# Layer 1's first operands beside projection 0's last block: SBUF pools laid out by the end of their place, PSUM pools kept over both parts

## The chip, the core and the metric

One Trainium2 chip, one of its cores. The metric is the device time of one execution in microseconds (us); lower is better. In the profile PE is TensorE, DVE VectorE, ACT ScalarE, POOL GpSimd and SP the engine that issues the DMAs.

## The reference

One inference step of a two-layer backbone over 128 prompt and 2048 latent tokens, width 1024. What matters here is the end of layer 0 and the start of layer 1:

```python
h = rmsnorm(x, norm_g[l]) * (1.0 + scale) + shift
# l == 0: gated linear attention heads | spatial-gating heads -> out (T x 1024)
# l == 1: pooling mixer heads | short gated convolution heads -> out (T x 1024)
out = out @ w_out[l]
x = x + gate * out
```

Layer 0's output projection ("projection 0") gives x after layer 0; layer 1 normalizes that x, multiplies it with an input projection of 1024 x 3072, mixes, and projects again.

## The kernel before, in words

Everything is kept channel-major: 128 channels on the partitions, tokens along the free axis. A float32 product is made from two halves, a rounded high part and the remainder (lines 206 to 208: ACT copies the high half, DVE or POOL subtracts for the low half), and three matmuls each (line 238).

Projection 0 (`out0`, line 1050) goes over five blocks of tokens (`BLKO`, line 31), called blocks 0 to 4 here: 512, 512, 512, 384 and 256 tokens. A block has eight output columns `c` of 128 channels; each takes 24 matmuls into one PSUM bank `ps_g`, DVE empties the bank into `xs_y` (line 1059), ACT squares it, POOL adds the squares (line 292), and a DMA writes `d_x1`. After a block, its inverse root mean square goes to `d_r` (line 1068). The weights of columns 0 to 2 lie in pool `wp`, those of columns 3 to 7 in `wr`. The operands of a block, `oh` and `ol`, lie in pool `oA` (blocks 0, 2, 4) or `oB` (blocks 1, 3). They are finished in tiles of 128 tokens by `finish_o` (line 911) while the block before is multiplied: load, add the state's product, sum of squares on TensorE (lines 270, 271), `newton` (lines 262 to 266), scale (lines 967, 968), split (line 971). Every tile but tile 0 also needs a state from the scan backwards (line 905).

Layer 1 (`block`, line 1446) goes over four blocks of 544 tokens, last tokens first, so that its first block needs x of tokens 1624 to 2175 only, which projection 0 has written with its second block. `operand` (line 1146) makes the block's operands: per `k` of 4 it loads two pieces `xk` of `d_x1`, scales them with `r` (line 372), adds the shift on ACT (line 1160), forms four differences `T` on POOL and DVE (line 1172) and splits seven tiles `t` into halves, 28 in all. The product is a Winograd form of seven products for each pair of weight rows (`Pair`, line 1378): m1, m2, m5, m6 of a pair, with m7, m4, m3 of the pair before between them. Then the output projection of the block (lines 1511 to 1538), whose banks line 1529 empties.

The order on each engine is set by the framework's scheduler from the program's dependences. A tile of a pool that is opened later waits only for those tiles of the closed pools on whose bytes it lies (`reuse_waits="tile"`). So where a pool lies decides when its first tile may be written. In the program before, `xk` lies on `oB`; the 28 tiles `t` lie on `oB` (10 of them), `wr` and a part of `xs`; `r` and `T` lie on the last `y` and `x` tiles of `xs`, which are in use to the end of projection 0. The PSUM pools `ps2` (4 banks `g`, 2 `m`, 2 `s`) and `ps3` (6 banks `g`, 2 `s`) follow each other.

Of the kernel before, what the change touches and what calls it, by code (L numbers as in the profile page):

```python
# [10 lines left out]
F32 = mybir.dt.float32  # L11
# [18 lines left out]

BLKO = [(1664, 2176), (1152, 1664), (640, 1152), (256, 640), (0, 256)]
NBO = len(BLKO)
# [54 lines left out]
def kernel(ctx: ExitStack, tc: tile.TileContext, xT, cT, w_ada, b_ada, norm_g, final_g,  # L87
# [29 lines left out]
    def const(src, shape, tag, dt=F32, pl=None):  # L117
        t = (pl or cst).tile(shape, dt, tag=tag)
        load(out=t, in_=src)
        return t  # L120

    def mtile():

        return ps.tile([P, 2, 512], F32, tag="m", bufs=banks[0])

    def btile():
        return (ps.tile([P, 512], F32, tag="m", bufs=2) if banks[0] == 1 else mtile()[:, 0, :])

# [782 lines left out]
    def finish_o(bi):  # L911
# [8 lines left out]
        def ob_part():  # L920
            for hh in range(4):
                hi, lo = o_tile(n, bi % 2)
                x = (xs.tile([P, WOP], F32, tag="x", bufs=2) if bi else
                     tmp.tile([P, 640], F32, tag="px", bufs=2))[:, 0:n]
# [101 lines left out]
    s2 = ExitStack()  # L1026
    ps = pool("ps2", space=PSUM, stack=s2, reuse_waits="tile")
    banks[:] = BANKS2
    opools.append(pool("oB", stack=s2, reuse_waits="tile"))
    wr = pool("wr", stack=s2, reuse_waits="tile")  # L1030
    xs = pool("xs2", stack=s2, reuse_waits="tile")
    tmp = pool("tmp2", stack=s2, reuse_waits="tile")
    width[:] = [512, 0, 0, 0, 3, 6]

# [3 lines left out]
    def w_out0(c):  # L1038
        if c == len(wres):
            if c < NHI:  # L1040
                wres.append(load_w(wo[0, c], KT * P))
            else:
                raw = raw_tile()[:, 0:KT * P]
                load(out=raw, in_=wo[0, c])
                hi, lo = (wr.tile([P, KT * P], F32R, tag=f"{z}{c}") for z in "hl")
                split(raw, hi, lo)
                wres.append((hi, lo))
        return wres[c]
# [36 lines left out]
    s3 = ExitStack()  # L1085
    ps = pool("ps3", space=PSUM, stack=s3, reuse_waits="tile")
    banks[:] = BANKS3
    wh = pool("wh", stack=s3, reuse_waits="tile")
    ring = pool("ring2", stack=s3, reuse_waits="tile")
    tmp = pool("tmp3", stack=s3, reuse_waits="tile")  # L1090
    c3 = pool("c3", stack=s3, reuse_waits="tile")
    late = ExitStack()
    o1 = pool("o1", stack=late, reuse_waits="tile", right=True)
# [50 lines left out]
    kept = [None]  # L1144

    def operand(bi, c0, w):

        jw = w - HALF
        r = tmp.tile([P, 560], F32, tag="r", bufs=1)[:, 0:w]
        load(out=r, in_=d_r[:, c0:c0 + w])  # L1150
        B = {n: [] for n in ("B11", "B21", "T1", "B22", "T2", "T3", "T4")}
        cn = cond_ranges(c0, c0 + w)
        for k in range(4):
            h = []
            for kk in (k, k + 4):
# [23 lines left out]
    def in1(bi, o8, fill):  # L1179
# [107 lines left out]
        def pair_pool(hh):  # L1287
# [17 lines left out]
            def c12(x, y):  # L1305
# [12 lines left out]
                for s0_, sn, off, lft, rgt in own_segs:  # L1318
# [59 lines left out]
        class Pair:  # L1378
# [67 lines left out]
    def block(bi):  # L1446
# [218 lines left out]
```

## Time and profile before

| | |
|---|---|
| median of 3 runs | 1901.35 us (1898.92 to 1901.35) |
| the profiled execution's own time | 1904.74 us |
| its span | 1902.9 us |
| TensorE busy | 1756.3 us, 92% of the span |
| VectorE busy | 1193.6 us, 63% |
| ScalarE busy | 842.0 us, 44% |
| GpSimd busy | 745.8 us, 39% |
| DMA engines | 69.3% of 16 engines' span |

The durations below come from the one profiled execution; 1.8 us lie around its span, and its time is 3.4 us above the median. TensorE is busy nearly everywhere, so the places where it is not are what to look for. The span in slices shows where they are, the stretches show how much they cost, the chain and the timelines show what they wait for.

### The profile page before, as it was taken

To read this page: it belongs to the slowest core of one execution; us is meant where nothing else is said; L and a number is where in the kernel's file an instruction comes from. 1 tells how busy PE (TensorE), PEld (TensorE's weight loads), DVE (VectorE), ACT (ScalarE), POOL (GpSimd) and SP (SyncE) were. 2 spreads that over 40 slices of the span, in tenths; PEclk is the share of its full clock that TensorE was granted. 3 is DMA by queue.
4 is the path that set the end of the run, shared out by engine and by line. 5 is a ranking of instruction groups with operands and counts; after the bars stand their busy time and mean duration, and the time that the engine had idled before them with its cause. 6 is when DMAs were issued, how large, how long until landed. Compare 5 with 4: busy or idle time off the path is not lost.

```text
span 1902.9 us, 39872 instructions
## 1 busy us (share of the span) xinstructions
PE 1756.3 (92%) x15115; PEld 1595.2 (84%) x15115; DVE 1193.6 (63%) x2262; ACT 842.0 (44%) x1783; POOL 745.8 (39%) x796
## 2 busy tenths in 40 slices
PE   5998999989988998998899959999999999999996
PEld 3886778768876987987678949988999999999996
DVE  4657853882588348646775456585768476837663
ACT  3545542542454436434444444454445254534431
POOL 0432433550474223244554343354346334532322
PEclk9999899989988999999899969999999999999998
DMA  8767796878867574475755367777877597759762
GB/s 310 269 234 244 271 319 225 280 270 285 284 227 247 205 264 148 145 210 174 218 168 162 111 199 251 247 246 241 313 266 253 177 325 250 235 180 327 236 213 98
DMA packets 232319, 443.76 MB, mean 233 GB/s; under 512 B 26176, under 2 KB 69056, under 8 KB 232128
## 3 DMA queue, kind: packets, MB, share of 16 engines
q1 hardware_dynamic: 232128, 441.22, 69.3%
q8 instruction: 119, 1.95, 0.4%
q14 instruction: 72, 0.59, 0.1%
HBM read 344.44 MB, written 96.68 MB: 232 GB/s over the span
## 4 chain that ended last, share of the span: by engine, by line
PE 59%; DVE 18%; DMA 12%; issue 4%; ACT 3%; SPq 2%; POOL 1%; DVEq 0%; ACTq 0%; POOLq 0%
PE ps_g L238 54%; DVE gl_Z L546 2%; DVE ring_xk L372 2%; DMA wp_raw<-in_w0c_dram 2%; DVE ring_t L208 2%; DMA wa_wa<-in_w_ada_dram 1%; DVE gl_L L535 1%; DMA dr_hl<-tmp_px 1%; DMA ring_xk<-dr_x 1%; DVE oA_Sb L905 1%; DMA oA_Sb<-dr_ub 1%; PE ps_s L338 1%; PE ps_s L1335 1%; DVE wp_raw L735 1%; DVE gl_A L598 1%
## 5 line engine op out<-in xcount | busy, mean ns | idle before, releaser
L238 PE MATMUL ps_g<-ring_t,wh_hi 128*128 128x272 f32 (+1 forms) x2688 | 525.7, 295 | 20.1 <-ACT ring_t L207 12.4
L238 PEld LDWEIGHTS ps_g<-ring_t,wh_hi 128*128 128x128 f32 x2688 | 428.7, 191 | 26.7 <-ACT ring_t L207 13.6
L238 PE MATMUL ps_g<-ring_t,wh_lo 128*128 128x272 f32 (+1 forms) x1344 | 387.9, 293 | 0.7 <-DVE wh_lo L208 0.7
L238 PEld LDWEIGHTS ps_g<-ring_t,wh_lo 128*128 128x128 f32 x1344 | 254.5, 191 | 1.5 <-DVE wh_lo L208 1.2
L238 PE MATMUL ps_g<-ring_hh,wp_hi 128*128 128x512 f32 (+2 forms) x632 | 239.1, 378 | 11.1 <-DVE tmp_ev L847 5.8
L238 PE MATMUL ps_g<-ring_hh,wp_lo 128*128 128x512 f32 (+2 forms) x632 | 235.3, 372 | 4.8 <-DVE wp_lo L208 3.9
L238 PE MATMUL ps_g<-ring_hl,wp_hi 128*128 128x512 f32 (+2 forms) x632 | 234.0, 370 | 0.0
L207 ACT ACTIVATE wh_hi<-wh_raw 128x512 fp32r<-128x512 f32 x208 | 130.7, 629 | 209.1 <-PE ps_g L238 175.5
L292 POOL TENSOR_TENSOR tmp_acc<-tmp_acc,tmp_px 128x512 f32<-128x512 f32 (+6 forms) x83 | 112.1, 1351 | 154.6 <-ACT tmp_px L291 152.7
L208 DVE TENSOR_TENSOR wh_lo<-wh_raw,wh_hi 128x512 fp32r<-128x512 f32 x156 | 125.5, 808 | 64.9 <-ACT wh_hi L207 50.4
L238 PE MATMUL ps_g<-wp_hi,ring_hh 128*128 128x256 f32 (+1 forms) x528 | 157.3, 299 | 8.2 <-DMA wp_hi<-dr_w8h 3.4
L238 PE MATMUL ps_g<-wp_lo,ring_hh 128*128 128x256 f32 (+1 forms) x528 | 152.5, 290 | 1.2 <-DMA wp_lo<-dr_w6l 0.8
L238 PE MATMUL ps_g<-wp_hi,ring_hl 128*128 128x256 f32 (+1 forms) x528 | 152.2, 290 | 1.1 <-DVE ring_hl L388 1.1
L238 PE MATMUL ps_g<-o_oh,wh_hi 128*128 128x272 f32 (+2 forms) x512 | 147.0, 292 | 5.9 <-ACT o_oh L207 5.9
L546 POOL TENSOR_TENSOR gl_Z<-gl_Z 128x128 f32<-128x128 f32 x170 | 84.0, 512 | 173.7 <-DVE gl_Z L546 106.4
L238 PE MATMUL ps_g<-o_ol,wh_hi 128*128 128x272 f32 (+2 forms) x512 | 149.5, 293 | 1.5 <-DVE o_ol L208 1.4
L238 PEld LDWEIGHTS ps_g<-ring_hh,wp_hi 128*128 128x128 f32 x632 | 123.9, 196 | 31.8 <-DVE tmp_ev L847 6.2
L238 PE MATMUL ps_g<-o_oh,wh_lo 128*128 128x272 f32 (+2 forms) x512 | 149.2, 292 | 0.8 <-DMA wh_lo<-dr_wo 0.8
L238 PEld LDWEIGHTS ps_g<-ring_hh,wp_lo 128*128 128x128 f32 x632 | 123.3, 195 | 24.3 <-DVE wp_lo L208 5.3
L238 PEld LDWEIGHTS ps_g<-ring_hl,wp_hi 128*128 128x128 f32 x632 | 123.7, 196 | 16.0 <-issue 1.2
L530 ACT ACTIVATE gl_L<-gl_Z 128x256 f32<-128x256 f32 x204 | 83.2, 418 | 110.8 <-DVE gl_Z L546 83.3
L238 PEld LDWEIGHTS ps_g<-wp_hi,ring_hh 128*128 128x128 f32 x528 | 101.7, 193 | 15.1 <-ACT ring_hh L387 4.0
(280 smaller groups left out, 3910.1 us busy)
## 6 DMA issues: line engine op xcount, KB each, us to landing
wh_raw<-in_w_dram SPq DMA_DIRECT2D x144, 256.0 KB, 3.6
wh_hi<-dr_hl SPq DMA_DIRECT2D x144, 256.0 KB, 3.3
wh_lo<-dr_hl SPq DMA_DIRECT2D x144, 256.0 KB, 3.7
wp_raw<-in_w_ada_dram SPq DMA_DIRECT2D x32, 512.0 KB, 5.1
wp_raw<-in_w_dram SPq DMA_DIRECT2D x24, 512.0 KB, 5.1
wh_raw<-dr_s SPq DMA_DIRECT2D x48, 256.0 KB, 3.8
wh_hi<-dr_wo SPq DMA_DIRECT2D x48, 256.0 KB, 3.7
wh_lo<-dr_wo SPq DMA_DIRECT2D x48, 256.0 KB, 4.1
```

The lines of the kernel that those rows point to most:

```text
L207: act(out=hi, in_=src, func=AF.Copy)
L208: (eng or lo_engine()).tensor_tensor(out=lo, in0=src, in1=hi.bitcast(F32), op=ALU.subtract)
L238: mm(out=out, lhsT=a, rhs=b, start=start and i == 0, stop=stop and i == n - 1, skip_group_check=resumed)
L292: eng.tensor_tensor(out=acc, in0=acc, in1=sq, op=ALU.add)
L338: mm(out=acc[32 * g:32 * g + 32, 0:w], lhsT=sc[:, k, :], rhs=wt[:, g * w:(g + 1) * w], start=k == 0, stop=k == KT - 1, tile_position=(0, 3 ...
L372: dve.scalar_tensor_tensor(out=xt[:, a:b], in0=xt[:, a:b], scalar=gs[:, l, k, cd:cd + 1], in1=r[:, a:b], op0=ALU.mult, op1=ALU.mult)
L530: act(out=dst.rearrange("p (b t s) -> p t b s", t=2, s=s), in_=diag_ap(Z, 2 * i, s), func=AF.Exp, scale=1.0 / 16.0)
L535: dve.tensor_tensor(out=L, in0=qk, in1=L, op=ALU.mult)
L546: (dve if i >= 2 or s < 4 else gps).tensor_tensor(out=dst, in0=dst, in1=bc(src), op=ALU.add)
L598: dve.copy_predicated(out=A[rr_, :, rr_], mask=notl[rr_].unsqueeze(1).to_broadcast([32, 4, 32]), data=D[rr_])
L735: dve.tensor_tensor(out=lo, in0=s_, in1=hi.bitcast(F32), op=ALU.subtract)
L905: dve.scalar_tensor_tensor(out=S[64:P, h, 0:P], in0=Sb[0][64:P, h, 0:P], scalar=S[64:P, h, P:P + 1], in1=S[64:P, h, 0:P], op0=ALU.mult, op ...
```

## The change

Blocks 3 and 4 of projection 0 become 256 and 384 tokens. Of the PSUM pools, `ps2` (4 banks `g`, 2 `s`) stays open through layer 1; the 2 banks for the states' products become a pool `pm` that closes with projection 0, and layer 1's third product bank `P3` takes their place as pool `px`; so layer 1 has 4 banks `g` and 2 `x` in place of 6 `g`. In SBUF, `wr` is split into one pool for each column 3 to 7, and layer 1's tiles `t` into five pools of 14, 3, 3, 4 and 4 tiles that lie in the same order: the 14 of `k` = 0 and 1 on `oB` (and a small buffer `xx`), the others on the weights of columns 3 and 4, 4, 5 and 6. `xk`, `r` and `T` go into a pool `e3` that lies on a pool closed long before. `U` and `s` lie on column 7's weights. The constants `c3` come to lie on the last statistics of projection 0. Statistics buffers `nw` in projection 0 go from 6 to 5, small edge buffers `ed` from 2 to 8.

```diff
-BLKO = [(1664, 2176), (1152, 1664), (640, 1152), (256, 640), (0, 256)]
+BLKO = [(1664, 2176), (1152, 1664), (640, 1152), (384, 640), (0, 384)]
...
-BANKS3 = (1, 2, 6)
...
+RINGS = (14, 3, 3, 4, 4)
...
+    pm = None
+
     def mtile():
 
-        return ps.tile([P, 2, 512], F32, tag="m", bufs=banks[0])
+        return (pm or ps).tile([P, 2, 512], F32, tag="m", bufs=banks[0])
...
     s2 = ExitStack()
-    ps = pool("ps2", space=PSUM, stack=s2, reuse_waits="tile")
+    s23 = ExitStack()
+    ps = pool("ps2", space=PSUM, stack=s23, reuse_waits="tile")
+    pm = pool("pm", space=PSUM, stack=s2, reuse_waits="tile")
...
-    wr = pool("wr", stack=s2, reuse_waits="tile")
+
+
+    xx = pool("xx", stack=s2, reuse_waits="tile")
+    wr = {c: pool(f"wr{c}", stack=s2, reuse_waits="tile") for c in range(NHI, KT)}
     xs = pool("xs2", stack=s2, reuse_waits="tile")
     tmp = pool("tmp2", stack=s2, reuse_waits="tile")
-    width[:] = [512, 0, 0, 0, 3, 6]
+    width[:] = [512, 0, 0, 0, 3, 5]
...
     s3 = ExitStack()
-    ps = pool("ps3", space=PSUM, stack=s3, reuse_waits="tile")
-    banks[:] = BANKS3
+    px = pool("px", space=PSUM, stack=s3, reuse_waits="tile")
     wh = pool("wh", stack=s3, reuse_waits="tile")
-    ring = pool("ring2", stack=s3, reuse_waits="tile")
+
+    rings = [(pool(f"t{i}", stack=s3, reuse_waits="tile"), n) for i, n in enumerate(RINGS)]
+    tu = pool("tu", stack=s3, reuse_waits="tile")
     tmp = pool("tmp3", stack=s3, reuse_waits="tile")
     c3 = pool("c3", stack=s3, reuse_waits="tile")
+    e3 = pool("e3", stack=s3, reuse_waits="tile")
...
-        r = tmp.tile([P, 560], F32, tag="r", bufs=1)[:, 0:w]
+        r = e3.tile([P, 560], F32, tag="r", bufs=1)[:, 0:w]
...
-                x = xk_tile(w)
+                x = e3.tile([P, 552], F32, tag="xk", bufs=3)[:, 0:w]
...
-            t = {n: ring.tile([P, 2, JW], F32R, tag="t", bufs=28) for n in B}
+            t = {n: t_tile(7 * k + i) for i, n in enumerate(B)}
...
-                self.P3 = gtile()
+                self.P3 = px.tile([P, 512], F32, tag="x", bufs=2)
```

The scheduler makes another order from it. First the engine VectorE before the change, around the last tile of `finish_o` in block 3 (tile 0; `xs_y` are block 3's columns, `tmp_nw` and `f_o` the tile's statistics and product, `oA_ol` its low halves):

```order
L263 TENSOR_SCALAR tmp_nw_12326<-ps_s_12319 128x512
L1059 SCALAR_TENSOR_TENSOR xs_y_12444<-ps_g_12446,cst_ada_98,xs_y_12444 128x384
L266 SCALAR_TENSOR_TENSOR tmp_nw_12326<-tmp_nw_12327,tmp_nw_12326 128x512
L968 SCALAR_TENSOR_TENSOR f_o_12312<-tmp_nw_12326,f_G_12314 128x512
L208 TENSOR_TENSOR oA_ol_12181<-f_o_12312,oA_oh_12180 128x128
L208 TENSOR_TENSOR oA_ol_12185<-f_o_12312,oA_oh_12184 128x128
L208 TENSOR_TENSOR oA_ol_12187<-f_o_12312,oA_oh_12186 128x128
L1059 SCALAR_TENSOR_TENSOR xs_y_12476<-ps_g_12478,cst_ada_98,xs_y_12476 128x384
```

The same tile on VectorE after the change, from block 3's last column on (lines are two further on here; `e_xk`, `e_T` and `t_t` are layer 1's pieces, differences and operand tiles); the three `oA_ol` of the tile follow three rows behind the last one shown:

```order
L1066 SCALAR_TENSOR_TENSOR xs_y_12526<-ps_g_12528,cst_ada_98,xs_y_12526 128x256
L265 TENSOR_SCALAR tmp_nw_12376<-ps_s_12369 128x512
L210 TENSOR_TENSOR t_t_12952<-e_xk_12944,t_t_12952 128x272
L210 TENSOR_TENSOR t_t_12955<-e_xk_12948,t_t_12955 128x272
L210 TENSOR_TENSOR t_t_12954<-e_T_12959,t_t_12954 128x272
L1187 TENSOR_TENSOR e_T_12962<-e_xk_12948,e_T_12960 128x272
L210 TENSOR_TENSOR t_t_12957<-e_T_12961,t_t_12957 128x272
L374 SCALAR_TENSOR_TENSOR e_xk_12985<-e_xk_12985,cst_gs_99,e_r_12942 128x544
L210 TENSOR_TENSOR t_t_12989<-e_xk_12981,t_t_12989 128x272
L268 SCALAR_TENSOR_TENSOR tmp_nw_12376<-tmp_nw_12377,tmp_nw_12376 128x512
L374 SCALAR_TENSOR_TENSOR e_xk_13018<-e_xk_13018,cst_gs_99,e_r_12942 128x544
L1187 TENSOR_TENSOR e_T_12997<-e_xk_12985,e_T_12996 128x272
```

Tile 0's rows have moved from before block 3's last two columns to behind its last column, and nine rows of layer 1's operands now stand among them.

TensorE at the end of projection 0 before the change (`oA`, `wr`: its last column; `ps_s_12822`: its sum of squares; `ring_t`, `wh`: layer 1's first products):

```order
L238 MATMUL ps_g_12790<-oA_oh_12206,wr_l_10_11144 128x256
L270 MATMUL ps_s_12822<-tmp_nw_12823,cst_ones_r_75 128x256
L271 MATMUL ps_s_12822<-tmp_nw_12824,cst_ones_r_75 128x256
L238 MATMUL ps_g_13055<-ring_t_12911,wh_hi_13058 128x272 x2
L238 MATMUL ps_g_13055<-ring_t_12911,wh_lo_13059 128x272
L238 MATMUL ps_g_13076<-ring_t_12912,wh_hi_13079 128x272
L238 MATMUL ps_g_13096<-ring_t_12913,wh_hi_13099 128x272
```

And after it (`t_t` in place of `ring_t`):

```order
L240 MATMUL ps_g_12808<-oA_oh_12172,wr_l_11162 128x384
L240 MATMUL ps_g_13096<-t_t_12952,wh_hi_13099 128x272 x2
L240 MATMUL ps_g_13096<-t_t_12952,wh_lo_13100 128x272
L240 MATMUL ps_g_13096<-t_t_12989,wh_hi_13099 128x272 x2
L240 MATMUL ps_g_13096<-t_t_12989,wh_lo_13100 128x272
L240 MATMUL ps_g_13096<-t_t_13026,wh_hi_13099 128x272 x2
```

The two matmuls of the last sum have moved behind layer 1's first 48 products, and the first product is done whole, `k` after `k`, where before three products were begun side by side.

## Rows read from the trace of the kernel before

**Rows 1.** The page's slices: the span in 40 equal parts of 47.6 us, one digit each, for TensorE's busy share and for the clock granted to it (tenths of full speed).

```profile
PE   5998999989988998998899959999999999999996
...
PEclk9999899989988999999899969999999999999998
```

**Rows 2.** The timeline of TensorE at the boundary: start (us), duration, engine, line, operation, what is written and read, count, and in brackets the idle time before it and what ended it.

```profile
1104.16 0.28 PE L238 MATMUL ps_g<-oA_oh,wr_l 128*128 128x256 f32 x1
...
1118.99 0.59 PE L238 MATMUL ps_g<-ring_t,wh_hi 128*128 128x272 f32 x1 [10.77 <-ACT ring_t L207]
...
1147.67 0.40 PE L238 MATMUL ps_g<-ring_t,wh_lo 128*128 128x272 f32 x1 [0.69 <-DVE wh_lo L208]
```

**Rows 3.** A stretch of 10 us inside the boundary, and one of 50 us behind it: start and end, length, busy time and instructions (x) of TensorE, its weight loads, VectorE, ScalarE and GpSimd, then granted clock, DMA share and GB/s.

```profile
1110.00:1120.00 10.00, 0.59 (x1) 0.29 (x1) 3.50 (x6) 2.83 (x6) 1.90 (x3) 0.50 0.57 205
...
1150.00:1200.00 50.00, 50.00 (x397) 49.85 (x396) 28.58 (x54) 23.68 (x46) 12.48 (x16) 1.00 0.76 248
```

**Rows 4.** The same columns for the stretch from 1106 to 1148 us, of the instructions alone that read or write layer 1's operand tiles (`ring_t`).

```profile
1106.00:1148.00 42.00, 21.85 (x76) 17.85 (x77) 11.42 (x16) 9.99 (x28) 12.05 (x12) 0.55 0.54 176
```

**Rows 5.** The chain that ended last, in order of time, at the boundary: start, duration, what.

```profile
1106.88 4.14 DMA yp_ys<-dr_x
...
1111.09 5.24 DMA tmp_r<-dr_r
...
1121.14 3.96 DMA ring_xk<-dr_x
...
1131.14 2.67 DMA ring_xk<-dr_x
```

**Rows 6.** The timeline of VectorE through the last two blocks of projection 0, columns as in rows 2.

```profile
1049.57 0.62 DVE L1059 SCALAR_TENSOR_TENSOR xs_y<-ps_g,cst_ada,xs_y 128x384 f32<-128x384 f32 x1 [1.57 <-PE ps_g L238]
...
1071.82 0.69 DVE L263 TENSOR_SCALAR tmp_nw<-ps_s 128x512 f32<-128x512 f32 x1 [2.60 <-ACT tmp_nw L262]
...
1074.42 1.31 DVE L968 SCALAR_TENSOR_TENSOR f_o<-tmp_nw,f_G 128x512 f32<-128x512 f32 x1
...
1076.11 1.05 DVE L208 TENSOR_TENSOR oA_ol<-f_o,oA_oh 128x128 fp32r<-128x128 f32 x3 [0.38 <-ACT oA_oh L207]
...
1081.11 0.62 DVE L1059 SCALAR_TENSOR_TENSOR xs_y<-ps_g,cst_ada,xs_y 128x384 f32<-128x384 f32 x1 [3.42 <-PE ps_g L238]
...
1083.99 0.61 DVE L1059 SCALAR_TENSOR_TENSOR xs_y<-ps_g,cst_ada,xs_y 128x128 f32<-128x128 f32 x2 [2.26 <-PE ps_g L238]
...
1104.90 0.61 DVE L1059 SCALAR_TENSOR_TENSOR xs_y<-ps_g,cst_ada,xs_y 128x128 f32<-128x128 f32 x2 [2.69 <-DMA wh_raw<-in_w_dram]
```

**Rows 7.** The timeline of VectorE in the block before those: the first sum of its three tiles, the statistics that the second operand's scale comes from and the last tile's product.

```profile
1005.52 0.68 DVE L950 TENSOR_TENSOR f_o<-ps_m,f_o 128x512 f32<-128x512 f32 x1
...
1024.88 1.66 DVE L283 SCALAR_TENSOR_TENSOR tmp_r<-tmp_nw,tmp_nw 128x512 f32<-128x512 f32 x1
...
1038.09 0.69 DVE L968 SCALAR_TENSOR_TENSOR f_o<-tmp_nw,f_G 128x512 f32<-128x512 f32 x1
```

**Rows 8.** The timeline of ScalarE for tile 0, in the second last block.

```profile
1071.03 0.69 ACT L262 ACTIVATE tmp_nw<-ps_s,cst_eps 128x512 f32<-128x512 f32 x1 [1.19 <-PE ps_s L271]
...
1071.75 0.63 ACT L264 ACTIVATE tmp_nw<-tmp_nw 128x512 f32<-128x512 f32 x1
...
1075.76 0.91 ACT L207 ACTIVATE oA_oh<-f_o 128x128 fp32r<-128x128 f32 x4 [1.80 <-DVE f_o L968]
```

**Rows 9.** The making of the first operands by line and form, 1112 to 1146 us: line, engine, operation, tiles, shapes, count, then busy us, mean ns of one, and idle time before with what ended it.

```profile
L372 DVE SCALAR_TENSOR_TENSOR ring_xk<-ring_xk,cst_gs,tmp_r 128x544 f32<-128x544 f32 x8 | 7.7, 988 | 8.0 <-DMA tmp_r<-dr_r 5.8 <-DMA ring_xk<-dr_x 2.2
...
L208 DVE TENSOR_TENSOR ring_t<-ring_xk,ring_t 128x272 fp32r<-128x272 f32 x8 | 7.4, 932 | 0.0
...
L207 ACT ACTIVATE ring_t<-tmp_T 128x272 fp32r<-128x272 f32 x16 | 6.0, 418 | 6.9 <-DVE tmp_T L1172 6.9
...
L1172 DVE TENSOR_TENSOR tmp_T<-ring_xk,tmp_T 128x272 f32<-128x272 f32 x8 | 4.6, 570 | 1.2 <-POOL tmp_T L1172 0.7 <-ACT ring_xk L1160 0.5
...
L208 DVE TENSOR_TENSOR ring_t<-tmp_T,ring_t 128x272 fp32r<-128x272 f32 x8 | 4.3, 572 | 0.0
...
L208 POOL TENSOR_TENSOR ring_t<-tmp_T,ring_t 128x272 fp32r<-128x272 f32 x7 | 6.9, 985 | 0.4 <-ACT ring_t L207 0.3
```

**Rows 10.** Stretches of 2 us around a stall earlier in projection 0, columns as in rows 3.

```profile
906.00:908.00 2.00, 0.51 (x1) 0.19 (x1) 1.11 (x3) 1.92 (x7) 0.39 (x1) 0.95 0.99 342
...
916.00:918.00 2.00, 2.00 (x6) 1.54 (x6) 1.90 (x3) 0.17 (x1) 0.45 (x1) 0.50 0.62 215
...
918.00:920.00 2.00, 2.00 (x10) 1.64 (x9) 1.31 (x5) 1.90 (x6) 1.09 (x2) 0.99 0.44 103
```

**Rows 11.** Line 266 on VectorE (two inputs in SBUF) from 990 to 1082 us: shortest, median and longest duration in ns, first and last start.

```profile
L266 DVE SCALAR_TENSOR_TENSOR tmp_nw<-tmp_nw,tmp_nw x8: 692/1101/1773, 992.9 to 1073.3; 128x512 f32<-128x512 f32 x8
```

**Rows 12.** Line 1529, which empties the output projection's PSUM banks in layer 1: its forms, and what ended the idle time of VectorE before it (us, times).

```profile
L1529 DVE SCALAR_TENSOR_TENSOR yp_ys<-ps_g,cst_ada,yp_ys x48: 482/499/503, 1297.0 to 1703.1; 128x272 f32<-128x272 f32 x32, 128x268 f32<-128x268 f32 x16
...
L1529 DVE SCALAR_TENSOR_TENSOR yo_y<-ps_g,cst_ada,yo_y x24: 344/363/506, 1847.6 to 1885.9; 128x128 f32<-128x128 f32 x8, 128x148 f32<-128x148 f32 x8, 128x276 f32<-128x276 f32 x8
...
  PE ps_g L238: 91.2, 47
```

**Rows 13.** What TensorE waited for from 940 to 1106 us: waiting line, releaser, us in total, times, longest.

```profile
PE ps_s L271 <- DVE tmp_nw L208: 2.9, 2, 1.6
...
PE ps_s L270 <- ACT tmp_px L207: 1.5, 1, 1.5
```

More of the change, by code (lines that the diff above doesn't have):

```diff
@@ L120, in const @@
         return t
+    pm = None
     def mtile():
-        return ps.tile([P, 2, 512], F32, tag="m", bufs=banks[0])
+        return (pm or ps).tile([P, 2, 512], F32, tag="m", bufs=banks[0])
     def btile():
-        return (ps.tile([P, 512], F32, tag="m", bufs=2) if banks[0] == 1 else mtile()[:, 0, :])
+        return (pm.tile([P, 512], F32, tag="m", bufs=2) if pm else mtile()[:, 0, :])
     def stile():
@@ L922, in ob_part @@
                 hi, lo = o_tile(n, bi % 2)
-                x = (xs.tile([P, WOP], F32, tag="x", bufs=2) if bi else
+                x = (xx.tile([P, WOP], F32, tag="x", bufs=2) if bi else
                      tmp.tile([P, 640], F32, tag="px", bufs=2))[:, 0:n]
@@ L1044, in w_out0 @@
                 load(out=raw, in_=wo[0, c])
-                hi, lo = (wr.tile([P, KT * P], F32R, tag=f"{z}{c}") for z in "hl")
+                hi, lo = (wr[c].tile([P, KT * P], F32R, tag=z) for z in "hl")
                 split(raw, hi, lo)
@@ L1144, with t_tile @@
     kept = [None]
+    def t_tile(i):
+        for pl, n in rings:
+            if i < n:
+                return pl.tile([P, 2, JW], F32R, tag="t", bufs=n)
+            i -= n
     def operand(bi, c0, w):
         jw = w - HALF
-        r = tmp.tile([P, 560], F32, tag="r", bufs=1)[:, 0:w]
+        r = e3.tile([P, 560], F32, tag="r", bufs=1)[:, 0:w]
         load(out=r, in_=d_r[:, c0:c0 + w])
@@ L1161, in operand @@
                 h.append(x)
-            t = {n: ring.tile([P, 2, JW], F32R, tag="t", bufs=28) for n in B}
+            t = {n: t_tile(7 * k + i) for i, n in enumerate(B)}
             hi = {n: z[:, 0, 0:jw] for n, z in t.items()}
             lo = {n: z[:, 1, 0:jw] for n, z in t.items()}
-            raw = {n: tmp.tile([P, JW], F32, tag="T", bufs=3)[:, 0:jw] for n in ("T1", "T2", "T3", "T4")}
+            raw = {n: e3.tile([P, JW], F32, tag="T", bufs=3)[:, 0:jw] for n in ("T1", "T2", "T3", "T4")}
             b11, b12 = (h[0][:, a:a + jw] for a in (0, HALF))
@@ L1227, in s_tile @@
         def s_tile():
-            return tmp.tile([P, JW], F32, tag="s", bufs=2)
+            return tu.tile([P, JW], F32, tag="s", bufs=2)
         def plus(dst, x, y):
@@ L1325, in c12 @@
                             ed = edge[:, side_, hh, 0:en]
-                            z = tmp.tile([P, HALO], F32, tag="ed", bufs=2)[:, 0:en]
+                            z = tmp.tile([P, HALO], F32, tag="ed", bufs=8)[:, 0:en]
                             dve.tensor_tensor(out=z, in0=sw_[:, off - hw + e0:off - hw + e0 + en],
@@ L1388, in copy @@
             def copy(self):
-                z = tmp.tile([P, JW], F32, tag="U", bufs=4)[:, 0:self.m]
+                z = tu.tile([P, JW], F32, tag="U", bufs=4)[:, 0:self.m]
                 act(out=z, in_=self.P[:, 0:self.m], func=AF.Copy)
@@ L1540, in fin @@
         def fin():
-            r = tmp.tile([P, 560], F32, tag="r", bufs=1)[:, 0:n]
+            r = e3.tile([P, 560], F32, tag="r", bufs=1)[:, 0:n]
             finish_rstd(acc, n, r)
@@ L1555 @@
     s3.close()
+    s23.close()
     late.close()
```

## The prediction

> **What bounds the kernel now.** I read the slices first: TensorE stands at nine tenths or more almost everywhere, so TensorE's own work sets the time, and what can be won lies in its holes. The largest inside the span is the 24th slice, 1094 to 1142 us, with busy five tenths and a granted clock of six [rows 1]. That is the boundary between projection 0 and layer 1. TensorE's timeline there shows the edges: the last column's last product is over at 1104.4 us, the first product of layer 1 starts at 1119.0 after 10.8 us of idleness, and the last short wait ends at 1147.7 [rows 2]. In between TensorE is idle or stops and goes at half clock, 1.2 GHz [rows 3]. From 1106 to 1148 us it does 76 products of layer 1 [rows 4]; behind the boundary it does 397 in 50 us, 0.126 us each [rows 3]. So the 76 are worth 9.6 us, and layer 1 stands at 1148 where it would stand had it started at full pace at 1138.4. The hole costs 1138.4 - 1104.4 = 34.0 us.
>
> What it waits for is in the chain: a store and reload of x (4.1 us), then `r` (5.2 us), then scaling, differences, splits, and reloads of `xk` of 4.0 and 2.7 us [rows 5]. None of that needs the last blocks' results; `r` and `T` wait for their bytes.
>
> **The change part by part.** The order after it puts layer 1's first product right behind the last column. I count the time from the start of block 3, which is 1049.6 less one column. A 384 token column takes (1081.1 - 1049.6) / 7 = 4.5 us and a 256 token one (1104.9 - 1084.0) / 7 = 3.0 us [rows 6]; so block 3 starts at 1045.1, and eight columns are 36.0 or 23.9 us.
>
> Block 3 at 256 tokens: 23.9 us. But tile 2's finishing now lies in it with tiles 1 and 0, three in place of two, in two thirds of the time. In the block before, three tiles took 32.6 us from the first tile's sum to the last one's product [rows 7]. TensorE stands in order behind their sums. Lower bound nothing, since the waits for such sums were 4.4 us in the whole stretch from 940 to 1106 [rows 13]; upper bound 32.6 - 23.0 = 9.6 us, the old pace with only the time behind the first column. One statistics buffer fewer (5 for 6) works the same way and is in these bounds. I take 3.0, towards the lower bound, because block 3 before, with two tiles beside it, took no longer for each token (4.5 us for 384) than block 4 with none (3.0 for 256) [rows 6].
>
> The start of block 4: this is the new wait. Before, tile 0's statistics reached ScalarE at 1071.0 and its last low half was done at 1077.2, a chain of 6.1 us that ended well ahead of block 3's end [rows 6, 8]. Now the order has its rows behind block 3's last column, mixed with operand work, and none of block 4's columns can start without tile 0. The first 14 operand tiles lie on `oB`, which block 3 reads to its end, so their splits start just then. On VectorE from that moment to tile 0's scaled product: its first statistic 0.69, splits of 0.93 twice and 0.57 twice, two differences of 0.57, `xk` scaled twice at 0.99, another split 0.93, line 266 at 1.10 and line 968 at 1.31 [rows 6, 9, 11]: 10.2 us. The first of the two `xk` must be loaded after its buffer is given back by a split some 2 us in, a reload of 2.7 to 4.0 us [rows 5], of which some 1.5 us stand open behind the rows in front of it. With 0.4 us of ScalarE before the first split [rows 9] and 0.9 for tile 0's halves [rows 8] TensorE stands 13.0 us. Lower bound 5.4 us: the chain alone, 6.1 less the 0.7 us of products still left when its sum is issued. Upper bound 18 us, below. On ScalarE eight splits of 0.42 stand before the statistic that VectorE's line 266 needs, 3.3 us, inside the same time.
>
> The clock: after an idle stretch earlier in projection 0 the granted clock stood at 0.50 and six products took 2 us where ten did at 0.99 [rows 10], a loss of 0.8 us in each such 2 us. I take three of them behind the new stall, 2.3 us; bounds 0 and 4.6, twice that.
>
> Block 4 at 384 tokens: 36.0 us. The rest of the operand work lies beside it. VectorE has room: its work for all operands in the hole is 8 x 0.99 + 8 x 0.93 + 8 x 0.57 + 8 x 0.57 = 24.5 us [rows 9], a third of it done by then, beside eight evacuations of about one us. The last 14 tiles come free column by column; the four last, on column 6, must be made within the last column and the first three products, some 4.5 + 4.5 us, for 4 splits of at most one us on each engine. So at layer 1 I leave 1.5 us: column 7's bytes hold `U`, and the first sums wait for the last stores. Bounds 0 and 5.8, a quarter of the 23 us that the four steps `k` took before, should one come late.
>
> Loads moved forward on SP cost nothing: `r` now waits in block 2 for statistics that were made at 1024.9 to 1026.5 [rows 7] plus a store and a reload of 4.1 and 5.2 us [rows 5], some 1036 us. VectorE's queue behind that holds tile 4's and 3's scaling and evacuations; four banks give TensorE three columns of cover, and the third tile, done at 1038.1 to 1038.8 before [rows 7], is no longer there. Should that cover be gone, up to 7 us would be added to block 2. The edge buffers cost nothing, as VectorE is not what TensorE waits for there.
>
> PSUM in layer 1: pairs keep two generations of each bank, as before. The output projection has 4 banks for 6. Its 72 evacuations take 0.3 to 0.5 us, and VectorE sat idle for TensorE before 47 of them [rows 12], so it empties early. I take 0, with -3 to +6 us for a block's other rows, from the nature of those waits.
>
> Sum: 1045.1 + 23.9 + 3.0 + 13.0 + 2.3 + 36.0 + 1.5 = 1124.8 us, against 1138.4: 13.6 us less. The profiled execution's 1904.7 would become 1891.2; the median of the runs shown lies 3.4 us below it, so 1901.4 becomes **1887.8 us**.
>
> One rule speaks against it. Line 266, with both inputs in SBUF, took 0.69 to 1.77 us [rows 11], though its shape never changes. The Trainium skill, SBUF — State Buffer, section "Who interferes with whom", says that a VectorE instruction with two SBUF inputs and a GpSimd instruction that reads SBUF exclude each other, and the one that starts second waits. The spread agrees with it but does not show it alone. Most rows in the new wait are of that kind; this is the second rival.
>
> **The rivals.**
> First: tile 0 isn't late. The scheduler may have it ready as the first columns begin, with the wait 5.4 us, no half clock and no other wait: 1045.1 + 23.9 + 5.4 + 36.0 = 1110.4, a gain of 28.0, 1873 us. For it: with two tiles beside it block 3 lost nothing for each token. Against: the order has the operand rows in front of tile 0's.
> Second: the chain is longer still. If ten of the VectorE rows each wait half of a 0.99 us GpSimd split [rows 9], the wait is 18 us; with block 3's waits at 6 and 3.5 for the clock the sum is 1134.0, a gain of 4.4, 1897 us. For it: the spread of line 266. Against: the durations that I summed already hold such waits, since both engines were busy in the hole [rows 3].
> Third, slower: four banks are too few for layer 1's output projection, and every evacuation then holds TensorE up. At 0.5 us for each of 72 it costs 36 us, net 22 slower: 1924 us. It decides from 0.19 us for each (13.6 / 72). Against: the 47 idle times [rows 12], and projection 0 already runs on four.
> Fourth: the change doesn't do what it says. If the last tiles come free only when projection 0 has ended, the hole returns in part and takes back the 13.6 us: 1901 us. Against: the four late tiles are needed by the fourth product and later.
>
> **How the numbers follow.** Forecast (gain of 8 to 20): 0.48. First rival 0.20, second 0.20, third 0.06, fourth 0.06. The range leaves out the third and parts of the first and fourth: 1874 to 1900 us; the forecast's own is 1881 to 1893. About 0.2%, 3.8 us, is what a measurement of this kernel can tell from no change. Faster: 0.48 + 0.20 + 0.14 of the second, 0.82. Within 0.2%: 0.05 of the second and the fourth's 0.06, 0.11. Slower: the third and 0.01, 0.07.
>
> **What would show it.** Right: TensorE's timeline has no idle time above 2 us between the last column and layer 1's first product; the chain shows tile 0's line 970 and the splits of `t` at the start of block 4, with a wait of about 13 us and a clock of 0.50 behind it; block 3's sums show waits of some 3 us. Wrong: no stall at block 4 (first rival); a stall of 18 us or more with line 268 above 1.5 us (second); TensorE waits on VectorE's emptying line in layer 1 (third); idle time at layer 1's start released by splits of `t` (fourth).

## The result, and the profile after

The change made the kernel faster: 1888.39 us, median of four runs (1885.64 to 1891.16), beside 1901.35, median of four runs of the kernel before. The ratio is 0.9933, 95% interval 0.9915 to 0.9952, or 12.7 us (9.1 to 16.2) of 1901.35. The forecast was 1887.8 us. The profiled execution took 1887.35 us.

The page of the changed kernel, its span and, from its slices, TensorE's busy share and granted clock:

```profile
span 1885.6 us, 39832 instructions
...
PE   5998999989988998998889799989998999999996
...
PEclk9999999999998999999899899989999999999998
```

Against [rows 1], the slice that read 5, at clock 6, is gone. A 7 stands in the 23rd slice, at clock 8: a smaller hole has opened some 40 us earlier.

TensorE's timeline, columns as in [rows 2]: the end of block 3, the start of block 4, block 4's last product, and the first waits of layer 1.

```profile
1065.70 0.28 PE L240 MATMUL ps_g<-oB_oh,wr_l 128*128 128x256 f32 x1
...
1074.11 0.58 PE L272 MATMUL ps_s<-tmp_nw,cst_ones_r 128*128 128x256 f32 x1 [8.13 <-ACT tmp_nw L209]
...
1077.25 0.58 PE L273 MATMUL ps_s<-tmp_nw,cst_ones_r 128*128 128x256 f32 x1 [2.56 <-POOL tmp_nw L210]
...
1080.25 1.33 PE L240 MATMUL ps_g<-oA_oh,wp_hi 128*128 128x384 f32 x3 [2.42 <-ACT oA_oh L209]
...
1116.26 0.34 PE L240 MATMUL ps_g<-oA_oh,wr_l 128*128 128x384 f32 x1
...
1116.44 0.41 PE L240 MATMUL ps_g<-t_t,wh_hi 128*128 128x272 f32 x2
...
1121.76 0.52 PE L240 MATMUL ps_g<-t_t,wh_hi 128*128 128x272 f32 x2 [0.30 <-ACT tu_U L1405]
```

Layer 1's first product follows block 4's last one without a gap; in [rows 2] 14.8 us lay between the starts of the two, with 10.8 of idleness in one piece. The new hole lies at block 4's start: the three waits, 13.1 us together, with two short sums between them. These sums are of block 3's own statistics, which stand in TensorE's order ahead of block 4's products. The last wait is for tile 0's high half, which ScalarE makes right behind VectorE's line 970, so tile 0 sets the end of the hole:

```profile
1079.89 0.91 ACT L209 ACTIVATE oA_oh<-f_o 128x128 fp32r<-128x128 f32 x4 [0.74 <-DVE f_o L970]
```

VectorE shows what stood in front of tile 0, from its first statistic to its scaled product (line 268 was line 266 before, 970 was 968, 374 was 372):

```profile
1068.77 0.68 DVE L265 TENSOR_SCALAR tmp_nw<-ps_s 128x512 f32<-128x512 f32 x1
1069.37 1.72 DVE L210 TENSOR_TENSOR t_t<-e_xk,t_t 128x272 fp32r<-128x272 f32 x2
1071.02 0.96 DVE L210 TENSOR_TENSOR t_t<-e_T,t_t 128x272 fp32r<-128x272 f32 x1
...
1072.90 1.11 DVE L374 SCALAR_TENSOR_TENSOR e_xk<-e_xk,cst_gs,e_r 128x544 f32<-128x544 f32 x1
1073.93 1.51 DVE L210 TENSOR_TENSOR t_t<-e_xk,t_t 128x272 fp32r<-128x272 f32 x1
1075.36 1.26 DVE L268 SCALAR_TENSOR_TENSOR tmp_nw<-tmp_nw,tmp_nw 128x512 f32<-128x512 f32 x1
1076.54 1.24 DVE L374 SCALAR_TENSOR_TENSOR e_xk<-e_xk,cst_gs,e_r 128x544 f32<-128x544 f32 x1
...
1078.62 1.24 DVE L970 SCALAR_TENSOR_TENSOR f_o<-tmp_nw,f_G 128x512 f32<-128x512 f32 x1
```

Every `t_t` and `e_xk` row is layer 1's; between L265 and L970 they fill most of 9.2 us. The clock behind the hole, in stretches of 5 us (length, TensorE busy and instructions, clock, DMA share, GB/s):

```profile
1080.00:1085.00 5.00, 4.75 (x15) 0.50 0.41 111
1085.00:1090.00 5.00, 5.00 (x30) 1.00 0.08 26
```

15 products in 4.75 us where 30 take 5.00: 2.25 us lost at 1.2 GHz. And layer 1, of its operand tiles alone in the first row, columns as in [rows 3, 4]:

```profile
1106.00:1148.00 42.00, 30.70 (x240) 30.40 (x241) 3.68 (x6) 2.87 (x8) 4.92 (x5) 1.00 0.92 315
...
1150.00:1200.00 50.00, 50.00 (x398) 49.71 (x397) 31.02 (x60) 24.47 (x48) 18.07 (x20) 1.00 0.75 244
```

240 products by 1148 us at 0.126 us each put layer 1's start at full pace at 1117.9 us.

**A common zero.** Up to projection 0's first product TensorE, VectorE, ScalarE and GpSimd do the same rows in both programs (on SP the last few loads differ), and yet that product, the first of these starts, differs by 7.0 us (before, then after):

```profile
L238 PE MATMUL ps_g<-oA_oh,wp_hi x72: 278/394/502, 877.7 to 1089.5; 128*128 128x512 f32 x48, 128*128 128x256 f32 x24
```

```profile
L240 PE MATMUL ps_g<-oA_oh,wp_hi x72: 336/394/686, 870.7 to 1095.4; 128*128 128x512 f32 x48, 128*128 128x384 f32 x24
```

So of the 17.3 us between the two spans 7.0 are the executions', not the change's. The stages below are counted from that product, read from TensorE's timeline; "predicted" is the prediction's own sum less 877.7.

| stage, us | before | predicted | after |
|---|---|---|---|
| blocks 0 to 2 | 167.5 | 167.4 | 168.5 |
| block 3 | 35.7 | 26.9 | 26.8 |
| hole at block 4's start | 0 | 13.0 | 14.3 |
| block 4, with the slow clock | 23.5 | 38.3 | 36.3 |
| to layer 1's start at full pace | 34.0 | 1.5 | 1.3 |
| layer 1, to the span's end | 764.5 | 764.5 | 767.7 |
| sum | 1025.2 | 1011.6 | 1014.9 |

By the traces the change is worth 10.3 us, inside the measured interval.

### The profile page after: what moved, and what is told of

Read it like the earlier page. It is cut to its first block, busy times and chain, and to the rows that moved or that the text cites. A ratio compares the mean times of both kernels' runs of the same rounds, so it can differ in the third digit from the quotient of the medians.

```text
span 1885.6 us, 39832 instructions
## 1 busy us (share of the span) xinstructions
PE 1743.2 (92%) x15115; PEld 1586.8 (84%) x15115; DVE 1206.9 (64%) x2262; ACT 842.3 (45%) x1783; POOL 742.1 (39%) x796
## 5 line engine op out<-in xcount | busy, mean ns | idle before, releaser
L240 PE MATMUL ps_g<-t_t,wh_hi 128*128 128x272 f32 (+1 forms) x1920 | 369.8, 290 | 0.5 <-ACT tu_U L1405 0.5
L240 PEld LDWEIGHTS ps_g<-t_t,wh_hi 128*128 128x128 f32 x1920 | 300.9, 188 | 1.7 <-ACT tu_U L1405 1.0
L240 PE MATMUL ps_g<-t_t,wh_lo 128*128 128x272 f32 (+1 forms) x960 | 275.2, 289 | 0.2 <-DVE wh_lo L210 0.2
L240 PEld LDWEIGHTS ps_g<-t_t,wh_lo 128*128 128x128 f32 x960 | 179.8, 188 | 0.8 <-DVE wh_lo L210 0.4
L240 PE MATMUL ps_g<-o_oh,wh_hi 128*128 128x272 f32 (+2 forms) x512 | 150.2, 297 | 16.0 <-ACT o_oh L209 15.4
L240 PE MATMUL px_x<-t_t,wh_hi 128*128 128x272 f32 (+1 forms) x768 | 152.8, 291 | 1.3 <-DVE tmp_ev L1246 0.9
```

The costliest lines, as they stand in the source:

```text
L240: mm(out=out, lhsT=a, rhs=b, start=start and i == 0, stop=stop and i == n - 1, skip_group_check=resumed)
```

## The experiments

All twelve in one table, with the changed kernel (after) on top: the ratio to the kernel before, timed beside the run, with its 95% interval, and the span less the start of projection 0's first product, from each run's trace (before 1025.2, after 1014.9).

| run | ratio | interval | us from that product |
|---|---|---|---|
| after | 0.9933 | 0.9915 to 0.9952 | 1014.9 |
| edge | 0.9925 | 0.9904 to 0.9947 | 1011.6 |
| edge_u | 0.9932 | 0.9913 to 0.9950 | 1011.6 |
| edge_v | 0.9924 | 0.9903 to 0.9944 | 1012.2 |
| blk_back | 0.9904 | 0.9883 to 0.9926 | 1008.3 |
| only_blk | 1.0029 | 1.0013 to 1.0045 | 1031.6 |
| only_banks | 1.0057 | 1.0037 to 1.0077 | 1035.6 |
| psum_back | 0.9974 | 0.9959 to 0.9990 | 1019.9 |
| fillx | 0.9910 | 0.9893 to 0.9927 | 1008.0 |
| nw6 | 1.0088 | 1.0068 to 1.0107 | 1043.1 |
| pad | 1.0078 | 1.0054 to 1.0103 | 1042.5 |
| blk_both | 0.9987 | 0.9975 to 0.9999 | 1025.9 |
| blk_fillx | 0.9860 | 0.9837 to 0.9883 | 1001.7 |

### Is the hole made by the rows in front of tile 0? (edge, edge_u, edge_v)

The first run adds an edge that orders instructions on one engine and makes none wait for a result; `lasti[0]` is tile 0's last high copy on ScalarE:

```diff
+                if bi == NB2 - 1 and k == 0 and n == "B11":
+                    with tc.issue_after(lasti[0].ins):
+                        split(z, hi[n], lo[n], e)
```

> After with one ordering edge and nothing else: on ScalarE the first split of layer 1's operand (k = 0, B11) stands behind the four high copies of tile 0, so all operand splits follow tile 0. Theory A (the 15.7 us that TensorE stands at block 4's start are made by operand rows in front of tile 0's on ScalarE and VectorE, and the engines have idle time for that work later, 1086 to 1099 us): the stall falls to tile 0's own chain behind its last sum at 1065.27, some 5 to 6 us (0.67 + 0.63 + 0.63 + 1.3 + 1.0 + 0.9), the gain over after is 9 to 10 us, 1878 to 1880 us. Rival B (the chain of tile 0 is late by itself, held by GpSimd and the evacuations): the stall stays above 12 us, 1885 to 1889. Rival C (what is put off comes back): the stall falls, but idle time of the same size appears between block 4's last column and layer 1's first products, 1886 to 1890.

TensorE's timeline at block 4's start, and the next long wait:

```profile
1069.60 0.38 PE L273 MATMUL ps_s<-tmp_nw,cst_ones_r 128*128 128x256 f32 x1 [3.99 <-ACT tmp_nw L209]
...
1072.22 1.33 PE L241 MATMUL ps_g<-oA_oh,wp_hi 128*128 128x384 f32 x3 [0.31 <-ACT oA_oh L209]
...
1117.36 0.52 PE L241 MATMUL ps_g<-t_t,wh_hi 128*128 128x272 f32 x2 [3.66 <-ACT tu_U L1411]
```

With 1.35 us before the second sum, the waits are 5.65 us in place of 13.1, and the hole from block 3's end to block 4's first product is 6.6 us in place of 14.3: theory A for the hole. What is left is near the prediction's lower bound for tile 0's chain alone, 5.4 us. But the gain by the traces is 3.3 us, not 9 to 10, and the ratio can't be told from after's: rival C in part. 3.66 us return at layer 1's start, where TensorE waits for `U`, ScalarE's copy of a product out of its bank. The next run sought the cause of that on ScalarE; `firstu[0]` is the first copy U:

```diff
+                    with tc.issue_after(firstu[0].ins) if bi == NB2 - 2 and k < 2 else ExitStack():
+                        act(out=x[:, a:b], in_=x[:, a:b], func=AF.Identity, bias=ada[:, 1, kk, cd:cd + 1])
```

> The run with the ordering edge, and a second edge: on ScalarE the shift rows of the second layer-1 block's operand (k = 0, 1) stand behind the first copy U. Theory A (the 3.7 us that TensorE then waits for U at layer 1's start come from those rows in front of it, the same cause as at block 4): the wait falls below 0.7 us and the run is 3 to 4 us faster than the one edge alone, ratio to before 0.990 to 0.991. Rival B (U is late by itself or the rows come back at the end of the first layer-1 block): the wait moves there, ratio 0.992 to 0.993.

The wait for U stayed, 4.29 us. On ScalarE, column 7's square stands in front of U and waits for its evacuation; on VectorE that evacuation stands behind two scalings of the next operand's `xk`:

```profile
1119.28 0.52 ACT L294 ACTIVATE tmp_px<-xs_y 128x384 f32<-128x384 f32 x1 [3.56 <-DVE xs_y L1068]
```

```profile
1116.37 2.22 DVE L375 SCALAR_TENSOR_TENSOR e_xk<-e_xk,cst_gs,e_r 128x552 f32<-128x552 f32 x2
1118.51 0.73 DVE L1068 SCALAR_TENSOR_TENSOR xs_y<-ps_g,cst_ada,xs_y 128x128 f32<-128x128 f32 x2
```

So the second operand's rows may hold U up on VectorE, and not on ScalarE as theory A had it. The third run put line 375 behind that evacuation, `lastev[0]`:

```diff
+                with tc.issue_after(lastev[0].ins) if bi == NB2 - 2 else ExitStack():
+                    make_t(x, kk, 1, r, cn)
```

> The run with the ordering edge, and a second edge on VectorE in place of ScalarE: the rows that scale xk of the second layer-1 block (line 375) stand behind column 7's evacuation in block 4. In the run with two edges before, column 7's square on ScalarE waited 3.6 us for that evacuation, and U stood behind it. Theory A: the wait for U at layer 1's start falls from 3.7 us to below 1 us, the run is some 3 us faster than with one edge, ratio 0.990 to 0.992. Rival B (U waits for something else as well): the wait stays above 3 us, 0.992 to 0.994.

```profile
1120.29 0.52 PE L241 MATMUL ps_g<-t_t,wh_hi 128*128 128x272 f32 x2 [1.08 <-ACT tu_U L1413]
...
1131.30 0.74 PE L241 MATMUL ps_g<-t_t,wh_hi 128*128 128x272 f32 x4 [1.14 <-DMA wh_hi<-dr_hl]
```

U's wait fell to 1.08 us, but waits of 0.77 and 0.80 for block 4's sums and 1.14 for a weight stand beside it, 3.8 us together, and the time is the same. Theory A is right on what held U and wrong on the time: here TensorE found its next wait at once.

### The block sizes (blk_back, only_blk)

```diff
-BLKO = [(1664, 2176), (1152, 1664), (640, 1152), (384, 640), (0, 384)]
+BLKO = [(1664, 2176), (1152, 1664), (640, 1152), (256, 640), (0, 256)]
```

> After with the sizes of blocks 3 and 4 put back to 384 and 256 tokens, all pools as in after. Theory A: tile 0 is one of two tiles in a block of 36 us and is done early, so the stall at block 4's start goes (15.7 us); block 4 lasts 24 us in place of 36, and operand work of some 24.5 us of VectorE rows beside eight evacuations of 0.5 needs a little more: 2 to 6 us come back at layer 1's start. Net 9 to 13 us faster than after, 1875 to 1880. Rival B (the longer last block is what carries the change, since the last tiles come free with the last columns): 12 us or more of idle time at layer 1's start, 1886 to 1892.

No wait at block 4's start; block 4 ends 229.6 us after the common zero, 16.3 earlier than in after. The only long wait at layer 1's start:

```profile
1101.79 0.40 PE L240 MATMUL ps_g<-t_t,wh_hi 128*128 128x272 f32 x1 [3.20 <-DVE t_t L210]
```

Theory A is right on the mechanism: a block of 24 us was nearly cover enough. Of the 16.3 us, 5.8 go to the boundary, which now costs 7.1 (347 products by 1148 us put layer 1's start at full pace at 236.7; the granted clock stood at 0.76 from 1100 to 1105 us), and 3.9 to layer 1, whose first wait for `o_oh` (the high half of the output projection's operand) grew from 6.83 to 8.57; 6.6 remain. By the ratios it is 5.5 us better than after, less than the 9 expected, and the two intervals overlap. The sizes alone, put into the kernel before:

> Before with the sizes of blocks 3 and 4 alone as in after, 256 and 384 tokens. Theory A (three tiles beside a block of 24 us are too many even without operand rows): a stall of 5 to 7 us at block 4's start as in the run with the ordering edge, and the hole of 34 us stays: 4 to 8 us slower than before, 1905 to 1909. Rival B (the longer last block by itself lets xk and a part of t, which lie on oB, be made in it): the hole shrinks by 10 us or more, 1890 to 1897.

```profile
1122.28 0.59 PE L238 MATMUL ps_g<-ring_t,wh_hi 128*128 128x272 f32 x1 [10.08 <-ACT ring_t L207]
```

Theory A holds: waits of 3.65, 1.19 and 0.31 us stand at block 4's start, the hole is as large as ever (3.13 us before the last sum and 10.08 before layer 1's first product), and the run is by the ratio 5.5 us slower. So the new sizes cost some 5.5 us by the ratios in either kernel, and the gain comes from the other edits: with `r` in another place it is gone (pad, below), and without the kept PSUM pools half of it or more is (psum_back, below). Which of the other SBUF places it needs (`e3`, the five pools of `t`, the pools of `wr`) no run here separates; nor was the number of edge buffers tried by itself.

### The PSUM banks (only_banks, psum_back, fillx)

```diff
-BANKS3 = (1, 2, 6)
+BANKS3 = (1, 2, 4)
...
+    px = pool("px", space=PSUM, stack=s3, reuse_waits="tile")
...
-                self.P3 = gtile()
+                self.P3 = px.tile([P, 512], F32, tag="x", bufs=2)
```

> Before with layer 1's banks alone as in after: 4 g and 2 x for P3 in place of 6 g; nothing of the boundary is touched. Theory A (the four g banks cost the 3 us by which after's span fell short of its boundary's gain): 3 us slower than before, 1904 to 1905, and TensorE's waits for o_oh at the three block ends grow to some 15 us in sum. Rival B (the 3 us come from the new places of U, s, r, xk and T, not from the banks): no change, 1900 to 1902.

Theory A is right in direction and three times too small: 10.4 us slower by the trace. TensorE's waits for o_oh in layer 1 (us in total, times, longest) in before, in this run and in after:

```profile
PE ps_g L238 <- ACT o_oh L207: 5.9, 3, 3.2
```

```profile
PE ps_g L238 <- ACT o_oh L207: 17.2, 3, 6.7
```

```profile
PE ps_g L240 <- ACT o_oh L209: 15.4, 4, 6.8
```

In after the same waits cost less: its layer 1 lost 3.2 us. The traces show what stands against them. Behind 1150 us TensorE's waits grew from 15.7 to 19.4 us in all: 9.5 more before o_oh, and less elsewhere, most of it before the product of the pooled rows (line 1335 before, 1350 after):

```profile
PE ps_s L1335 <- DVE tmp_ev L1320: 3.0, 3, 1.9
PE ps_s L1335 <- DVE tmp_ev L1329: 1.5, 1, 1.5
```

```profile
PE ps_s L1350 <- DVE tmp_ev L1335: 0.4, 1, 0.4
```

Which of its other edits does this wasn't tried. Then after with PSUM as before:

> After with PSUM as in before: layer 1 has its own pool with 6 g and 2 s banks, P3 out of g; SBUF pools and block sizes stay. Theory A (the kept PSUM pools buy layer 1's start ahead of block 4's statistics, and cost some 3 us in layer 1's output projection): TensorE's order has the two sums of block 4's statistics in front of layer 1's first product; they come some 7 us after the last column (1123.4 against 1116.6 in after), so 5 to 7 us of idle time there, and 3 us back in layer 1: 2 to 4 us slower than after, 1890 to 1893. Rival B (layer 1's loss isn't from the banks): 5 to 7 us slower, 1893 to 1896. Rival C (the sums cost nothing, since the operand is late anyway): 3 us faster, 1885.

```profile
1119.23 0.69 PE L272 MATMUL ps_s<-tmp_nw,cst_ones_r 128*128 128x384 f32 x1 [6.30 <-ACT tmp_nw L209]
```

The sum of block 4's statistics holds layer 1 up for 6.3 us, as theory A said; but little came back: the o_oh waits were still 11.6 us with six banks, so the banks make only a part of after's 15.4. By the trace 5.0 us slower than after, by the ratio 7.8: nearer to rival B. A direct test of the banks lends one out at a block's end, for products of the output projection that need only operands already made (the early products):

```diff
-                    first.append((halves(c), [gtile() for _ in groups]))
+                    first.append((halves(c), [px.tile([P, 512], F32, tag="x", bufs=2) if c and not i else gtile()
+                                              for i in range(len(groups))]))
```

> After with the early products of the output projection's column 1, first half, put into one of the two x banks, which are free at a block's end, in place of a g bank; nothing else. Theory A (at the end of a layer-1 block TensorE waits for o_oh since four g banks hold too few early products): each of the three waits for o_oh (6.8, 5.1 and 3.1 us in after) falls by about the 18 products that now stand in front of it, 18 x 0.125 = 2.3 us, some 6 us in sum, 1882 to 1884. Rival B (the waits are those for the last operand's chain, whatever stands in front): 18 products more in front, but the waits fall by less than 2 us in sum, 1887 to 1889.

```profile
PE ps_g L240 <- ACT o_oh L209: 9.4, 4, 4.3
```

The waits fell from 15.4 to 9.4 us, 6.0 less, as theory A expected of 18 products at each of three ends; the run is 6.9 us faster than after by the trace and 4.4 by the ratio, where the intervals overlap. Theory A holds: what four banks lack is room for early products.

### The sixth statistics buffer (nw6, pad, blk_both)

```diff
-    width[:] = [512, 0, 0, 0, 3, 5]
+    width[:] = [512, 0, 0, 0, 3, 6]
```

> After with six statistics buffers (nw) in projection 0 as in before, in place of five. Theory A (the missing buffer is what makes TensorE wait 3.2 and 3.3 us for sums in projection 0's first two blocks, at 903 and 977 us, with the half clock behind them): these waits shrink to below 1.7 us as in before, 2 to 4 us faster than after, 1884 to 1886. Rival B (the waits come from the operand rows of o and the wr splits, which stand in another order since the pools were split): the waits stay, 1887 to 1890.

The two waits stayed, 3.17 and 3.32 us, so they aren't the buffer's: rival B there. But the time went against both, 28 us slower than after by the trace. Layer 1's first product waits 11.65 us, because `r` comes late:

```profile
1125.35 0.59 PE L240 MATMUL ps_g<-t_t,wh_hi 128*128 128x272 f32 x1 [11.65 <-ACT t_t L209]
```

The loads of `r` in after and in this run, 1000 to 1150 us (count, ns, first and last start):

```profile
L1165 SPq DMA_DIRECT2D e_r<-dr_r x2: 320/324/327, 1023.2 to 1111.0; - x2
```

```profile
L1165 SPq DMA_DIRECT2D e_r<-dr_r x2: 319/348/376, 1119.0 to 1145.5; - x2
```

The first load starts some 95 us later. `r2`, projection 0's own row of inverse roots, is written last of all, by block 4. By the layout of the program, which no row of a profile shows, it ends 32 bytes ahead of `r` with five buffers; the sixth moves it 2,048 bytes on, so that it lies on the first 2,016 bytes of `r`. The next run tests whether that place alone decides, with a dead tile in place of the buffer:

```diff
+            if bi == 0:
+                gps.memset(tmp.tile([P, WOP], F32, tag="pad", bufs=1), 0.0)
             r = tmp.tile([P, WOP], F32, tag="r2", bufs=1)[:, 0:n]
```

> After with one dead tile of 2 KB put ahead of r2 in projection 0's pool and five statistics buffers as in after: r2, which block 4 writes last, then lies on the first 2,016 bytes of layer 1's r. Theory A (the run with six buffers was slower by place alone: layer 1's r is loaded only when block 4's r2 has been stored, and every operand row needs r): the same idle time at layer 1's start, 11 to 12 us before its first product and stop and go behind it; no operand rows beside block 4, so its stall at the start is 5 to 6 us; 1908 to 1918 us on the scale of before's 1899. Rival B (the sixth buffer itself, another order of the statistics, made that run slow): within 4 us of after, 1884 to 1892.

```profile
1070.76 1.33 PE L240 MATMUL ps_g<-oA_oh,wp_hi 128*128 128x384 f32 x3 [0.31 <-ACT oA_oh L209]
...
1124.69 0.59 PE L240 MATMUL ps_g<-t_t,wh_hi 128*128 128x272 f32 x1 [13.01 <-ACT t_t L209]
```

Theory A holds: the same loss without the buffer. Block 4's start waits only 5.3 us here (3.65 + 1.35 + 0.31), since no operand row stands in front of tile 0: the hole lies at one place or the other. The run that joined three changes carried the same late `r`:

> After with blocks of 384 and 256 tokens, six statistics buffers, and column 1's first half in an x bank. If the three are independent: the block sizes give 5.6 us over after (by the ratios 0.9904 and 0.9933), the buffers 2 to 4, the x bank 6: 1873 to 1877. If the waits at layer 1's block ends aren't of the banks (rival B of the run with the x bank): 1879 to 1882. If the sixth buffer moves the pools behind it so that an operand tile comes late: idle time of more than 5 us at layer 1's start.

It shows the last case, a wait of 13.26 us at layer 1's start, and 0.9987.

### The version that comes out (blk_fillx)

> After with blocks of 384 and 256 tokens and column 1's first half in an x bank, five statistics buffers. If the two gains add: after 0.9933, less 0.0029 for the block sizes (0.9904), less 0.0023 for the bank (0.9910): 0.988, 1876 us on the scale of before's 1899, with no stall at block 4, 3.2 us of waiting at layer 1's start, and 4.3, 2.9 and 1.9 us before o_oh at the block ends. If the first block end stays as long as with the block sizes alone (8.6 us and 2.8 us before the pooled rows), 0.990.

Block sizes as before the change, all its pools, five buffers, and the bank lent. The ratio is 0.9860: better than after, whose interval doesn't meet this one, and below both of its parts (the interval of blk_back touches it at 0.9883). TensorE's waits at layer 1's start and at the first block end:

```profile
1103.80 0.39 PE L240 MATMUL ps_g<-t_t,wh_hi 128*128 128x272 f32 x1 [3.21 <-DVE t_t L210]
...
1260.36 0.81 PE L240 MATMUL ps_g<-o_oh,wh_hi 128*128 128x268 f32 x2 [6.88 <-ACT o_oh L209]
```

The first end kept 6.9 us and not 4.3, as the second case had it; the other two fell to 2.8 and 1.9. The gains still add: 13.2 us over after by the traces, where the parts give 6.6 and 6.9; by the ratios it is 13.9, where they give 5.5 and 4.4.

## Why the prediction was right, point by point

- **The bound.** "The hole costs 1138.4 - 1104.4 = 34.0 us" and none of it needs the last blocks: right. 1.3 of the 34.0 us are left at that boundary in after, and where `r` alone is held back (pad), a hole returns.
- **Blocks 0 to 2**, taken as unchanged: 1.1 us longer than its 167.4. Block 1 took 58.5 us for 55.4, with a sum that waited 3.27 us at 977.7 while VectorE stood at a state's reload (1.37 us) in front of it; what made the reload late wasn't followed. The sixth statistics buffer doesn't (nw6). Block 2, a tile fewer, took 48.6 for 50.0, so the 7 us that loads moved forward might have added there didn't come.
- **Block 3, 23.9 + 3.0**: the sum is right to 0.1 us, the reason wrong. TensorE waited for nothing there. By its timeline the columns' products take 23.3 us and the three tiles' own products and the sums in TensorE's stream 3.5. The step that failed is "block 3 before, with two tiles beside it, took no longer for each token": at one digit a column the 2.2 us of such rows in that block can't be seen. The upper bound is also off: it takes 23.0 us as the time behind the first column, which by its own terms is 23.9 - 3.0 = 20.9.
- **Block 4, 36.0**: too large by the same step, since 4.5 us a column held tile products that block 4 has none of. Without the slow clock's 2.25 us it took 34.1.
- **The hole at block 4's start, 13.0**: 14.3, by the mechanism named, rows of layer 1 in front of tile 0: without them, in the run with the edge, it is 6.6. Not seen: block 3's own sums stand in TensorE's order before block 4's products; they end before tile 0's half is there.
- **The clock, 2.3**: 2.25 measured.
- **Layer 1's start, 1.5**: 1.3.
- **Layer 1, "I take 0"**: 3.2, inside its bounds. The step "it empties early" looked at evacuations, and TensorE waited for one once, 0.6 us. What the banks limit is how many early products can stand in front of the last operand; the lent bank shows it. That only 3.2 us were lost for 9.5 more before o_oh is luck in part: waits elsewhere in layer 1 fell, which the prediction didn't weigh.
- **"One statistics buffer fewer (5 for 6) works the same way"**: missed. The edit is no cost but the condition of the whole gain, as pad shows; as a place in SBUF it was not weighed.
- **The rivals.** The first, tile 0 in time, is what the old block sizes give. The second, a longer chain, did not come: the hole is 14.3 us and not 18, and line 268 of tile 0 took 1.26 us, under the 1.5 named as its sign. The third, evacuations that hold TensorE up, did not come. The fourth, operand tiles that come late, did not come in after and came in the runs with the late `r`.

The errors, +1.1, -0.1, +1.3, -2.0, -0.2 and +3.2, make 3.3 us: by the traces 10.3 us were gained where 13.6 were predicted. The errors of both signs partly cancel, and the medians, 13.0 apart, agree better than the steps do: that the forecast of 1887.8 us is met to 0.6 us is luck.

## What to carry to other kernels

When work is pulled forward beside a running block, look at what it stands in front of on each in-order engine: the hole moved from layer 1's start to block 4's, and only the old block sizes, with which tile 0 was done early and the operands had nearly enough cover, were rid of most of both. In a layout by the end of a place, check which tile is freed last and what lies on its bytes; here one buffer more in another pool undid the whole gain. And price a bank taken away by the early products that it held, not by the evacuations.

## What the runs showed that was not expected

- The start of projection 0's first product ranged from 865.2 to 877.7 us over 14 profiled executions in which TensorE, VectorE, ScalarE and GpSimd do the same rows up to it. The loads on SP don't explain it: they stand in one order in before (877.7), only_blk (873.3) and only_banks (865.2). Stages are better compared from a common product than from the start of the span.
- The slow clock cost about the same behind a hole of 14.3 us as behind one of 6.6: block 4 took 36.3 us behind the one and 36.6 behind the other; in the other five runs with a hole of some 6.3 us there it took 35.4 to 36.6. With the edge, stretches of 5 us from 1070 had clocks of 0.58 and 0.74, and 1.00 from 1080.
- Three rows of line 375 of one shape (128x552) took 0.78, 0.78 and 1.52 us in the second run with an edge, and 1.31, 1.54 and 1.62 in the third. GpSimd worked beside them, but no run here isolates the cause.
